# Attention's output projection by seven block products of eight, and the order of the rotation of q, k and v

## The chip, the cores and the metric

One core of one Trainium2 chip runs the whole program. The metric is the device time in microseconds (us) from start to end of one execution. The engines are PE (TensorE, the matrix products), ACT (ScalarE), DVE (VectorE), POOL (GpSimd) and SP (SyncE, which only issues DMA transfers here); each runs its own list of instructions in order and waits on the others through semaphores.

## The reference

Two sequences of 512 tokens with 1024 features go through two layers. The first mixes by a Fourier transform, the second by attention; each is followed by an MLP with squared ReLU. The part that matters here is the second layer's attention:

```python
def gqa_attention(h, w_qkv, q_gain, k_gain, w_o):
    qkv = h @ w_qkv
    q, k, v = split(qkv)     # 8 heads of q, 2 of k and v, 128 wide
    q = axial_rope(rms_norm(q, q_gain)) * HEAD_DIM ** -0.5
    k = axial_rope(rms_norm(k, k_gain))
    p = softmax(q @ k.T)               # per head, 512 x 512
    o = p @ v
    return o @ w_o           # the output projection, 1024 x 1024

x = x + gqa_attention(rms_norm(x, attn_norm), ...)
x = x + sq_relu_mlp(rms_norm(x, mlp_norm), w_up, w_down)
```

## The kernel before

**Precision.** Every float32 operand of a product is split into two float32r halves: ACT casts the high half, DVE subtracts it to get the low half (`split`, lines 84 to 86). A product of two split operands is three matmuls, high by high, high by low, low by high (`mm3`, lines 79 to 82, and `product`, line 801). All matmuls spoken of here have 128 rows, 128 columns and a moving side of 512.

**Buffers.** Five raw buffers of 512 KB take weights as they come from memory (`rawp`); four `w` buffers of 1 MB hold split weights (`wp`); 38 slots of 512 KB hold everything between stages (`act`, tiles named `u` in the profile); eight temporaries of 256 KB are named `t`; PE writes into eight PSUM banks named `ps`.

**Order.** Where the text says nothing else, a planner orders each engine's list: it takes the instructions in program order as priority and puts out those that are ready by its own costs, buffers included. Inside `tc.manual_schedule(engines=...)` the named engines keep program order.

**q, k and v** (from line 1385). Three column groups of `w_qkv`, in the order 2 (k and v), 0, 1 (q), by two sequences by four tiles of 128 tokens; each tile is 24 matmuls into one bank (`qkv`). For a tile ACT empties the bank (lines 1410, 1415), `norm_rope` (line 1301) squares each head with an accumulated sum (`head_squares`), takes the root in a chain of small DVE and ACT steps, then scales each head on ACT into a new tile (line 1315), multiplies by the two rotation tables on DVE (lines 1321, 1324) and adds on POOL (line 1326). All of that is written tile by tile: the whole of one tile's `norm_rope` stands before the next tile's. The four weights of a column group are loaded by SP into raw buffers and split (`load_w`), two of them into `w` buffers and two into slots (`lent`). The last two tiles of the last group are worked on during the first heads of attention.

**Attention** (from line 1421). For each of 16 heads (8 of each sequence): `scores` (12 matmuls, row maximum on DVE, exponential on ACT, scaling on POOL), `transpose_p` (16 transposes, then a split per bank), `values` (12 matmuls, then the head's output is split into `oT`). The next head's scores stand between the transposes of this one. During heads 6, 8, 10 and 12 the first four rows of `w_o` are loaded and split.

**Output projection** (from line 1451). For each half of the heads, for each sequence, for each of eight output blocks, `project` (line 785) makes 12 matmuls and DVE adds the bank to the residual (line 791). The residual of both sequences comes back from memory (`load_xs` from `park`). In the second half each finished block is squared on ACT (line 160) and added up on POOL (line 164), multiplied by the next norm's gain (line 206) and put away again (line 193). `blocks.root(0)` then sums the squares by small matmuls (line 172), `blocks.spread(0)` makes rows of the roots, and `blocks.first` and `first_lo` make the first operands of the second MLP.

**The second MLP** already uses the same form of block product that the change brings to the projection: `Blocks` holds 2 x 2 blocks (half of the features by sequence) under the names `b11`, `b21`, `b22`, `t1` to `t4`, and `second_sums` forms them.

## Time and profile before

The times shown are three runs and one profiled execution, all of the same kernel.

| | us |
|---|---|
| median of 3 runs | 1705.6 (1704.97 to 1710.73) |
| profiled execution | 1707.82 |
| its span in the profile | 1706.0 |
| PE busy | 1672.2 |
| DVE busy | 1233.7 |
| ACT busy | 866.0 |
| POOL busy | 358.1 |

The span is the time from the first to the last instruction that the profile shows; the execution's own time has a little around it. A row of a group names the line, the engine, the operation, output and input tiles, shapes, how many there were, the busy time, the mean duration of one in ns, and the idle time before them with what ended it. In a row of the order of time the first two numbers are start and length in us. The MATMUL rows overlap: PE starts the next before the last has ended. A row of waits reads: who waited, for whom, us in total, times, the longest.

### The profile page before, as it was taken

What the parts mean: (1) busy time and instruction counts of PE and PEld (TensorE: products, weight loads), DVE (VectorE), ACT (ScalarE), POOL (GpSimd) and SP (SyncE); (2) the same over time, 40 slices, a digit from 0 to 9 for tenths busy, and PEclk for the clock granted to TensorE, in tenths of its full rate; (3) what the DMA queues carried; (4) which work ended last, traced back from release to release, by engine and by line L of the source; (5) the groups of instructions that cost most, each with busy time, mean ns of one, the idle gap of its engine ahead of it and who ended that gap; (6) DMA issues with size and microseconds to landing.
All of it is one profiled execution on the core that took longest, in us unless ns stands there. A gap on an engine that the chain in (4) does not pass through costs nothing. (4 is left out here: it accounts for less than half of the span.)

```text
span 1706.0 us, 22195 instructions
## 1 busy us (share of the span) xinstructions
PE 1672.2 (98%) x7874; PEld 1393.4 (82%) x7874; DVE 1233.7 (72%) x1848; ACT 866.0 (51%) x1532; POOL 358.1 (21%) x332
## 2 busy tenths in 40 slices
PE   5999999999999999999999999999999999999998
PEld 4988888888888888788877888888888888887887
DVE  7869777546886869875588834687855477878875
ACT  6766445446443425456687714564444563433334
POOL 1320443231000001322234302103432220000002
PEclk8999999999999999999999999999999999999999
DMA  8652555449864757421000212234544696756632
GB/s 275 166 210 96 188 189 185 161 170 334 302 220 154 239 176 232 176 85 46 26 26 1 100 50 111 105 127 145 206 159 148 208 376 202 238 160 214 186 107 99
DMA packets 112863, 281.46 MB, mean 165 GB/s; under 512 B 11480, under 2 KB 12632, under 8 KB 112752
## 3 DMA queue, kind: packets, MB, share of 16 engines
q1 hardware_dynamic: 91520, 238.87, 39.7%
q0 software_dynamic: 6976, 15.21, 4.9%
q10 hardware_dynamic: 14256, 25.96, 4.0%
q8 instruction: 62, 1.02, 0.2%
q14 instruction: 49, 0.40, 0.1%
HBM read 204.96 MB, written 73.99 MB: 164 GB/s over the span
## 5 line engine op out<-in xcount | busy, mean ns | idle before, releaser
L807 PE MATMUL ps<-u,w 128*128 128x512 f32 x4656 | 1065.6, 389 | 2.2 <-DVE w L86 1.4
L807 PEld LDWEIGHTS ps<-u,w 128*128 128x128 f32 x4656 | 872.6, 188 | 186.8 <-DVE w L86 2.5
L85 ACT CAST w<-raw 128x1024 fp32r<-128x1024 f32 (+1 forms) x224 | 218.1, 980 | 342.6 <-PE ps L807 232.5
L86 DVE TENSOR_TENSOR w<-raw,w 128x1024 fp32r<-128x1024 f32 (+1 forms) x224 | 261.2, 1170 | 83.0 <-ACT w L85 82.7
L86 DVE TENSOR_TENSOR u<-u,u 128x1024 fp32r<-128x1024 f32 x134 | 161.3, 1232 | 18.1 <-ACT u L85 17.8
L85 ACT CAST u<-u 128x1024 fp32r<-128x1024 f32 x134 | 134.6, 1046 | 76.6 <-PE ps L807 38.1
L80 PE MATMUL ps<-u,u 128*128 128x512 f32 (+2 forms) x424 | 162.8, 385 | 2.5 <-DVE u L86 1.6
L81 PE MATMUL ps<-u,u 128*128 128x512 f32 (+2 forms) x424 | 157.3, 371 | 1.1 <-DVE u L86 1.0
L82 PE MATMUL ps<-u,u 128*128 128x512 f32 (+2 forms) x424 | 157.6, 372 | 0.4 <-DVE u L407 0.4
L1012 DVE TENSOR_TENSOR u<-ps,u 128x512 f32<-128x512 f32 x160 | 109.3, 685 | 36.6 <-PE ps L807 33.9
L807 PE MATMUL ps<-u,u 128*128 128x512 f32 x552 | 132.3, 390 | 1.9 <-DVE t L891 1.6
L922 POOL TENSOR_TENSOR u<-u 128x512 f32<-128x512 f32 x28 | 36.8, 1313 | 430.6 <-ACT u L821 430.6
L1041 POOL DMA_DIRECT2D raw<-w_sum x32 | 27.9, 873 | 470.0 <-DMA raw<-w_sum 155.5
L807 PEld LDWEIGHTS ps<-u,u 128*128 128x128 f32 x552 | 103.4, 188 | 24.5 <-issue 2.4
L164 POOL TENSOR_TENSOR t<-t,t 128x512 f32<-128x512 f32 (+1 forms) x52 | 76.3, 1473 | 202.5 <-ACT t L160 147.0
L820 ACT ACTIVATE t<-t 128x512 f32<-128x512 f32 x64 | 40.5, 632 | 112.9 <-DVE t L891 99.7
L80 PEld LDWEIGHTS ps<-u,u 128*128 128x128 f32 x424 | 82.8, 195 | 14.8 <-DVE u L86 2.0
L82 PEld LDWEIGHTS ps<-u,u 128*128 128x128 f32 x424 | 82.4, 194 | 14.0 <-DVE u L407 0.8
L81 PEld LDWEIGHTS ps<-u,u 128*128 128x128 f32 x424 | 82.8, 195 | 13.0 <-DVE u L86 2.9
L86 DVE TENSOR_TENSOR u<-ps,u 128x512 fp32r<-128x512 f32 (+4 forms) x126 | 76.6, 627 | 16.5 <-ACT u L85 15.2
L85 ACT CAST u<-ps 128x512 fp32r<-128x512 f32 (+4 forms) x126 | 66.2, 543 | 22.3 <-PE ps L82 13.7
L791 DVE TENSOR_TENSOR u<-ps,u 128x512 f32<-128x512 f32 (+1 forms) x48 | 30.9, 644 | 59.6 <-PE ps L82 59.6
(219 smaller groups left out, 1995.9 us busy)
## 6 DMA issues: line engine op xcount, KB each, us to landing
raw<-w_up SPq DMA_DIRECT2D x80, 512.0 KB, 4.5
u<-spill_t SPq DMA_DIRECT2D x60, 512.0 KB, 7.2
raw<-w_sum SPq DMA_DIRECT2D x56, 512.0 KB, 5.4
u<-spill_b SPq DMA_DIRECT2D x45, 512.0 KB, 6.2
spill_t<-u SPq DMA_DIRECT2D x84, 256.0 KB, 2.0
spill_b<-t ACTq DMA_DIRECT2D x60, 256.0 KB, 4.2
raw<-w_row SPq DMA_DIRECT2D x28, 512.0 KB, 5.3
park<-u SPq DMA_DIRECT2D x24, 512.0 KB, 3.4
```

What stands on the lines that cost most here:

```text
L80: nc.tensor.matmul(out, lh, rh, start=first, stop=False)
L81: nc.tensor.matmul(out, lh, rl, start=False, stop=False)
L82: nc.tensor.matmul(out, ll, rh, start=False, stop=last)
L85: nc.scalar.copy(dst_hi, src)
L86: eng.tensor_sub(dst_lo, src, f32(dst_hi))
L164: nc.gpsimd.tensor_add(acc[q][:, :n], acc[q][:, :n], s[:, :n])
L791: nc.vector.tensor_add(x[:, :n], o[:, :n], x[:, :n])
L807: nc.tensor.matmul(o, w[x][:, sl], h[k][y], start=first and k + i == 0, stop=k == n - 1 and i == 2, skip_group_check=not first)
L820: nc.scalar.activation(t, src, AF.Relu)
L922: eng.tensor_sub(t[:, 0], b12, b11)
L1012: nc.vector.tensor_add(x, o, x)
L1041: nc.gpsimd.dma_start(s[:, 1], w[:, 3], accum_op=ALU.add)
```

## The change

The projection is seen as a product of 2 x 2 blocks: the weights by parity of the output block and half of the heads, the heads' outputs by half of the heads and sequence. Instead of eight block products it makes seven, with sums and differences of the blocks on both sides (Winograd's form of Strassen's scheme), for each of four column groups.

- **Weights.** `keep` forms four sums for each column group, splits them in place and writes both halves to memory (`kept`); it is a generator of 17 steps, and one step stands after each tile of q, k and v from the second on. `load_kept` brings them back: of its 14 tiles the first four are loaded and split as before during attention, two (`w_a22`, laid out by the host) are loaded and split in the projection, and eight come ready from `kept` straight into a `w` buffer, in two transfers each.
- **Heads' outputs.** `values` copies each output from its bank as float32 on ACT; for sequence 0 it also splits it. `plain_sums` forms and splits the other five operands.
- **Projection.** Three parts, with PE's order fixed: eight products with sequence 0's two halves, in a turning order over the column groups; twelve with t2, t3, t4; eight with t1 and b22. What several outputs share is collected in four tiles `e` and added to the residuals by POOL's adding DMA (`common`).
- **Rotation.** A tile's squares and root are issued at once, its scaling and rotation only after the next tile's squares (`turned`). The scaling now writes in place, which frees one temporary; the last tile before attention has a slot for it.

```diff
@@ -152,15 +152,15 @@
     def xt(q, fo):
         return xs[q, fo // 2][:, fo % 2]
 
-    def square(q, fo, n=512, alone=False):
-
-        if fo == 0:
+    def square(q, fo, n=512, alone=False, first=0):
+
+        if fo == first:
             acc[q] = tm()
-        s = tm() if fo else acc[q]
+        s = acc[q] if fo == first else tm()
         nc.scalar.activation(s[:, :n], xt(q, fo)[:, :n], AF.Square)
         if alone:
             apart[q] = s
-        elif fo:
+        elif fo != first:
             nc.gpsimd.tensor_add(acc[q][:, :n], acc[q][:, :n], s[:, :n])
 
     def sums(q, n=NT):
@@ -201,7 +201,7 @@
             self.g0, self.f, self.r, self.rows, self.b = g0, {}, {}, {}, {}
 
         def gain(self, q, fo):
-            if fo % 2 == 0:
+            if (q, fo // 2) not in self.f:
                 self.f[q, fo // 2] = slot([P, 2, 512], F32)
             nc.scalar.activation(self.f[q, fo // 2][:, fo % 2], xt(q, fo), AF.Copy,
                                  scale=gc[:, self.g0 + fo : self.g0 + fo + 1])
@@ -233,6 +233,34 @@
         def first_lo(self, i):
             h = self.b["b11" if i < 2 else "b21"][i % 2]
             nc.vector.tensor_sub(h[1], self.f[0, i], f32(h[0]))
+
+        def plain_sums(self):
+
+            f, t1, t2 = self.f, [], []
+            for c in range(2):
+                t1.append(slot([P, 2, 512], F32))
+                t2.append(slot([P, 2, 512], F32))
+                nc.vector.tensor_sub(t1[c], f[1, c], f[0, c])
+                nc.vector.tensor_sub(t2[c], f[1, 2 + c], t1[c])
+                self.put("t2", t2[c])
+                yield
+            for c in range(2):
+                nc.vector.tensor_sub(f[1, c], f[1, 2 + c], f[1, c])
+                self.put("t3", f[1, c])
+                yield
+            for c in range(2):
+                nc.vector.tensor_sub(f[0, 2 + c], f[0, 2 + c], t2[c])
+                self.put("t4", f[0, 2 + c])
+                yield
+            for c in range(2):
+                self.put("t1", t1[c])
+                yield
+            for c in range(2):
+                self.put("b22", f[1, 2 + c])
+                yield
+
+        def operand(self, name):
+            return [(h[0][:, i], h[1][:, i]) for h in self.b[name] for i in range(2)]
 
         def second_sums(self):
 
@@ -808,8 +836,7 @@
                                  stop=k == n - 1 and i == 2, skip_group_check=not first)
 
     def first_product(l, blocks, rows, ahead):
-        def b(name):
-            return [(h[0][:, i], h[1][:, i]) for h in blocks.b[name] for i in range(2)]
+        b = blocks.operand
 
         def put(op, p, src, queue):
             for g, (p0, n) in enumerate(GROUPS[l]):
@@ -1310,10 +1337,10 @@
         yield
         for h0 in range(0, n, step):
             t = ts[h0 // nh]
-            x, t1, t2 = [tm((P, step, HD)) for _ in range(3)]
+            t1, t2 = [tm((P, step, HD)) for _ in range(2)]
+            x = raw[:, h0 * HD : (h0 + step) * HD].rearrange("p (h d) -> p h d", h=step)
             for i in range(step):
-                nc.scalar.activation(x[:, i], raw[:, (h0 + i) * HD : (h0 + i + 1) * HD],
-                                     AF.Copy, scale=r[:, h0 + i : h0 + i + 1])
+                nc.scalar.activation(x[:, i], x[:, i], AF.Copy, scale=r[:, h0 + i : h0 + i + 1])
 
             def every(ap):
                 return ap.unsqueeze(1).broadcast_to([P, step, ap.shape[-1]])
@@ -1327,7 +1354,8 @@
                                      t1[:, i : i + 2], t2[:, i : i + 2])
             yield
 
-    vt, kr, kT, qr, oT = {}, {}, {}, {}, {}
+    vt, kr, kT, qr = {}, {}, {}, {}
+    heads_out, ahead = Blocks(None), []
 
     def transpose_k(q):
         for h in range(NKV):
@@ -1375,15 +1403,83 @@
         for sc in range(NT):
             vh, vl = vt[q][0][:, sc, c : c + HD], vt[q][1][:, sc, c : c + HD]
             mm3(o, vh, vl, pts[sc][:, 0], pts[sc][:, 1], sc == 0, sc == NT - 1)
-        t = slot([P, 2, 512], F32R)
-        split(t[:, 0], t[:, 1], o)
-        oT[q, h] = t
+        i, j = h // 2, h % 2
+        name = "b11" if h < 4 else "b21"
+        if j == 0:
+            heads_out.f[q, i] = slot([P, 2, 512], F32)
+            if q == 0:
+                heads_out.b.setdefault(name, []).append([slot([P, 2, 512], F32R) for _ in range(2)])
+        nc.scalar.copy(heads_out.f[q, i][:, j], o)
+        if q == 0:
+            hi, lo = heads_out.b[name][-1]
+            split(hi[:, j], lo[:, j], o)
+
+
+
+    kept = [drm.tile([4, P, 2, 512], F32, name=f"kept_{m}") for m in range(4)]
+
+    def load_parts(m):
+        r = [rawp.tile([P, 1024], F32R, tag="raw", name=nm("raw")) for _ in range(2)]
+        for i in range(2):
+            nc.sync.dma_start(f32(r[i]), w_o[m, 1 - i])
+        return r
+
+    def keep():
+
+        r = load_parts(0)
+        yield
+        for m in range(4):
+            x1, x2, y1, y2 = [x[:, i : i + 512] for x in r for i in (0, 512)]
+
+            def put(i, x):
+                h = tm((P, 512), F32R)
+                split_in_place(h, x)
+                nc.sync.dma_start(kept[m][i][:, 0], f32(h))
+                nc.gpsimd.dma_start(kept[m][i][:, 1], f32(x))
+
+            def add(out, a, b, op=ALU.subtract):
+                nc.vector.tensor_tensor(out=f32(out), in0=f32(a), in1=f32(b), op=op)
+
+            add(y1, y1, x1)
+            add(x1, x1, x2, ALU.add)
+            put(0, x1)
+            yield
+            add(x2, x2, y1)
+            put(2, y1)
+            yield
+            add(y2, y2, x2)
+            put(1, x2)
+            yield
+            put(3, y2)
+            if m < 3:
+                r = load_parts(m + 1)
+            yield
+
+    def split_in_place(h, x):
+        nc.scalar.copy(h, f32(x))
+        nc.vector.tensor_sub(x, f32(x), f32(h))
+
+    def load_kept():
+
+        i = len(ahead)
+        if i < 4:
+            w = load_w(w_o[i, 0], nc.vector, 2)
+        elif i in (8, 9):
+            w = load_w(w_a22[i - 8])
+        else:
+            t = wp.tile([P, 2, 1024], F32R, tag="w", name=nm("w"))
+            for j in range(2):
+                m, k = (2 * (i % 2) + j, i // 2 - 1) if i < 8 else (i - 10, 3 * j)
+                nc.sync.dma_start(f32(t)[:, :, j * 512 : j * 512 + 512], kept[m][k])
+            w = t[:, 0], t[:, 1]
+        ahead.append([(w[0][:, i : i + 512], w[1][:, i : i + 512]) for i in (0, 512)])
 
 
     transposes = {(2, 1, 3): 0, (0, 0, 3): 1}
 
     begun = [qkv(2, 0, t, wkv, 0, KC - 2) for t in range(NT)]
     token_scale(0)
+    keeping, turned = keep(), iter(())
     for cg in (2, 0, 1):
         ws = wkv if cg == 2 else [load_w(w_qkv[cg, u], home=own if u < 2 else lent) for u in range(4)]
         for q in range(NSEQ):
@@ -1411,11 +1507,15 @@
                     split_scaled(vt[q][0][:, t], vt[q][1][:, t], o[:, 256:], r)
                     todo = norm_rope(raw, NKV, rt["k"], [t], [kr[q][:, t]])
                 else:
-                    raw = tm()
+                    raw = slot([P, 512], F32) if (cg, q, t) == (1, 1, 1) else tm()
                     nc.scalar.activation(raw, o, AF.Copy, scale=r)
                     todo = norm_rope(raw, 4, rt["q"], [t], [qr[q, 2 * cg + i][:, t] for i in range(2)])
-                for _ in todo:
+                next(todo)
+                for _ in turned:
                     pass
+                turned = todo
+                if cg != 2 or q or t:
+                    next(keeping, None)
 
 
     heads = [(q, h) for q in range(NSEQ) for h in range(NH)]
@@ -1425,11 +1525,13 @@
     nc.scalar.activation(raw[:, :512], o, AF.Copy, scale=rs[1][:, 2:3])
     head_squares(raw, 0, 4, ss)
     qT = transpose_q(*heads[1])
+    for _ in turned:
+        pass
     o = qkv(1, 1, 3, ws)
     nc.scalar.activation(raw[:, 512:], o, AF.Copy, scale=rs[1][:, 3:4])
     todo = norm_rope(raw, 4, rt["q"], [2, 3], [qr[1, 2 + i][:, t] for t in (2, 3) for i in range(2)],
                      ss, 2, nc.gpsimd)
-    ahead = []
+    assert next(keeping, 0) == 0
     for n in range(1, len(heads) + 1):
         pts, nxt = [], []
         for t in range(NT):
@@ -1446,32 +1548,83 @@
             head_squares(raw, 4, 4, ss)
         probs = nxt
         if n in (6, 8, 10, 12):
-            ahead.append(load_w(w_o[len(ahead)], nc.vector, 2))
+            load_kept()
 
     blocks = Blocks(2 * KC)
     nc.scalar.activation(one[:, :1], last[:, :1], AF.Sqrt)
-    for kh in range(2):
-        ahead += [load_w(w_o[k], home=lent) for k in range(len(ahead), 4 * kh + 4)]
-        ws = ahead[4 * kh :]
-        for q in range(NSEQ):
-            if kh == 0:
-                load_xs(q, park[q])
-            for fo in range(KC):
-                project(q, fo, ws, [(oT[q, 4 * kh + k][:, 0], oT[q, 4 * kh + k][:, 1]) for k in range(4)])
-                if kh == 0:
-                    continue
-                square(q, fo, alone=(q, fo) == (0, KC - 1))
-                blocks.gain(q, fo)
-                if fo % 2:
-                    put_away(q, fo // 2)
-                if (q, fo) == (1, 0):
-                    blocks.root(0)
-                if (q, fo) == (1, 2):
-                    blocks.spread(0)
-                if (1, 2) < (q, fo) < (1, 7):
-                    blocks.first(fo - 3)
-                if (q, fo) > (1, 3):
-                    blocks.first_lo(fo - 4)
+
+
+    todo, e = heads_out.plain_sums(), [tm() for _ in range(4)]
+    load_xs(0, park[0])
+
+    def add(x, o):
+        nc.vector.tensor_add(x, o, x)
+
+    def common(m, *xs):
+        for x in xs:
+            nc.gpsimd.dma_start(x, e[m], accum_op=ALU.add)
+
+    def turn(*steps):
+
+        for i in range(5):
+            if i < 4:
+                yield i, 0
+            if i:
+                yield i - 1, 1
+
+    with tc.manual_schedule(engines={ET.PE}):
+        o = {}
+        for m, i in turn():
+            if i == 0:
+                o[m] = ps()
+            product(o[m], ahead[m][i], heads_out.operand(("b11", "b21")[i]), i == 0)
+            if i:
+                add(xs[0, m][:, 0], o[m])
+                load_kept()
+            else:
+                nc.scalar.copy(e[m], o[m])
+            if m + i > 1:
+                next(todo)
+        load_xs(1, park[1])
+        for k, name in enumerate(("t2", "t3", "t4")):
+            h = heads_out.operand(name)
+            for m in range(4):
+                o = ps()
+                product(o, ahead[4 + 2 * k + m // 2][m % 2], h)
+                if k < 2:
+                    add(e[m], o)
+                    common(m, *((xs[1, m][:, 0],), (xs[0, m][:, 1], xs[1, m][:, 1]))[k])
+                else:
+                    add(xs[0, m][:, 1], o)
+                if k:
+                    fo = 2 * m + k - 1
+                    square(0, fo, alone=fo == KC - 1)
+                if k == 2:
+                    blocks.gain(0, 2 * m)
+                    blocks.gain(0, 2 * m + 1)
+                    put_away(0, m)
+                if m % 2:
+                    load_kept()
+                next(todo, None)
+        o = {}
+        for j, (m, i) in enumerate(turn()):
+            if i == 0:
+                o[m] = ps()
+            product(o[m], ahead[10 + m][i], heads_out.operand(("t1", "b22")[i]), i == 0)
+            fo = 2 * m + 1 - i
+            add(xt(1, fo), o[m])
+            square(1, fo, first=1)
+            blocks.gain(1, fo)
+            if i:
+                put_away(1, m)
+            if j == 0:
+                blocks.root(0)
+            if j == 2:
+                blocks.spread(0)
+            if 1 < j < 6:
+                blocks.first(j - 2)
+            if 2 < j < 7:
+                blocks.first_lo(j - 3)
     second_product(1, blocks, ())
     ats = []
     for f in range(2 * PLAIN):
@@ -1711,7 +1864,7 @@
...
-        "w_o": i["attn_w_o"][0].reshape(KC, P, D),
+        "w_o": i["attn_w_o"][0].reshape(2, 4, P, 4, 2, P).transpose(3, 4, 2, 0, 1, 5).reshape(4, 2, P, 1024),
+    arrays["w_a22"] = arrays["w_o"][:, 1, :, 512:].reshape(2, 2, P, 512).transpose(0, 2, 1, 3).reshape(2, P, 1024)
```

4 lines of the change are left out of this document (2 added, 2 removed).

## The prediction

> **What bounds the kernel now.** I read the page's head first, then the waits of TensorE (PE) from the end of the first MLP to the start of the second, then the busy time by stage, and last the order of time at the seams.
>
> ```profile
> span 1706.0 us, 22195 instructions
> PE 1672.2 (98%) x7874; PEld 1393.4 (82%) x7874; DVE 1233.7 (72%) x1848; ACT 866.0 (51%) x1532; POOL 358.1 (21%) x332
> ...
> PE ps L81 <- DVE u L86: 1.0, 3, 0.5
> PE ps L80 <- ACT u L85: 0.3, 1, 0.3
> PE ps L1367 <- POOL t L1361: 0.2, 1, 0.2
> ...
> 739.00:766.00 27.00, 27.00 (x128) 22.55 (x127) 18.69 (x75) 17.24 (x68) 4.41 (x6) 1.00 0.06 20
> 766.00:858.00 92.00, 92.00 (x415) 76.23 (x414) 54.32 (x167) 63.58 (x239) 26.11 (x34) 1.00 0.10 35
> 858.00:870.00 12.00, 12.00 (x70) 10.03 (x69) 10.37 (x22) 9.62 (x22) 3.52 (x5) 1.00 0.27 89
> 870.00:900.00 30.00, 28.83 (x154) 22.46 (x153) 25.30 (x60) 26.06 (x66) 13.05 (x19) 1.00 0.01 1
> 900.00:930.00 30.00, 29.64 (x166) 23.81 (x166) 26.59 (x57) 23.22 (x55) 12.88 (x20) 1.00 0.00 1
> 930.00:967.00 37.00, 37.00 (x211) 31.08 (x210) 30.90 (x67) 28.65 (x68) 13.10 (x19) 1.00 0.11 33
> 981.00:1073.00 92.00, 92.00 (x417) 76.41 (x416) 44.05 (x59) 31.79 (x48) 15.81 (x11) 1.00 0.22 80
> ```
>
> Columns of the stages: stretch, length, busy us of PE, PEld, DVE, ACT, POOL, granted clock, DMA share, GB/s. The first two rows are q, k and v, the next four attention, the last the output projection. PE is never idle in q, k, v and the projection, at clock 1.00, and loses 1.17 and 0.36 us in two stretches of attention. So a matmul taken out of the projection shortens the end by its whole slot, unless something else comes late; work taken off DVE or ACT there is worth nothing by itself.
>
> **What is removed.** The projection has 2 halves x 2 sequences x 8 outputs x 4 heads x 3 = 384 matmuls. The new form has 4 column groups x 7 products x 4 x 3 = 336, of the same shape: 48 fewer.
>
> ```profile
> 1046.11 0.39 PE L80 MATMUL ps<-u,u 128*128 128x512 f32 x1
> ...
> 1051.32 0.39 PE L82 MATMUL ps<-u,u 128*128 128x512 f32 x1
> ```
>
> From the first to the second of these lie 23 matmul steps: 5.21 / 23 = 0.2265 us a slot (the 0.39 overlaps its neighbours). 48 x 0.2265 = **10.9 us** off the path; with 12 matmuls a product takes 2.72 us.
>
> **What is added in q, k and v.** For each of four column groups: two loads of 512 KB, four DVE sums, four ACT casts, four DVE remainders, four writes of 256 KB on SP's queue and four on POOL's.
>
> ```profile
> 1037.57 0.68 DVE L859 TENSOR_TENSOR raw<-raw,raw 128x512 f32<-128x512 f32 x1
> 809.16 0.61 ACT L85 CAST w<-raw 128x512 fp32r<-128x512 f32 x1
> L1041 POOL DMA_DIRECT2D raw<-w_sum x32: 858/868/907, 418.1 to 1607.5; - x32
> ```
>
> 32 x 0.68 = 21.8 us of DVE, 16 x 0.61 = 9.8 of ACT, 16 x 0.868 = 13.9 of POOL. The first two stage rows hold 119 us; there DVE goes from 73.0 to 94.8 (80%), ACT from 80.8 to 90.6 (76%), POOL from 30.5 to 44.4. PE waits for none of it: it only needs its bank emptied by one ACT copy a tile, and eight banks stand against one tile every 24 x 0.2265 = 5.4 us. I cost it at nothing; the cover is those banks and PE's full row. The rotation put behind the next tile's squares issues the same instructions 5.4 us later, fills ACT's and DVE's waits for each other, and gains nothing, since PE has no idle time there to win.
>
> The seam is where the weights of the next column group must be ready, because the sums now share the five raw buffers and SP's queue with them.
>
> ```profile
> L94 SPq DMA_DIRECT2D raw<-w_qkv x8: 328/328/382, 694.0 to 735.4; - x8
> ...
> 764.59 1.37 DVE L86 TENSOR_TENSOR u<-raw,u 128x1024 fp32r<-128x1024 f32 x1
> 766.85 1.23 DVE L86 TENSOR_TENSOR u<-raw,u 128x1024 fp32r<-128x1024 f32 x1 [0.41 <-ACT u L85]
> ...
> 769.43 0.39 PE L80 MATMUL ps<-u,u 128*128 128x512 f32 x1
> 770.79 0.39 PE L80 MATMUL ps<-u,u 128*128 128x512 f32 x1
> ...
> raw<-w_o SPq DMA_DIRECT2D x8, 512.0 KB, 4.3
> L85 ACT CAST u<-u 128x1024 fp32r<-128x1024 f32 x134 | 134.6, 1046 | 76.6 <-PE ps L807 38.1
> L86 DVE TENSOR_TENSOR u<-u,u 128x1024 fp32r<-128x1024 f32 x134 | 161.3, 1232 | 18.1 <-ACT u L85 17.8
> ```
>
> The third and fourth weights are split at 764.59 + 1.37 = 765.96 and 768.08 and used at 769.43 and 770.79: 3.5 and 2.7 us to spare, with raws that lay ready since before 740. Parts 0 and 1 stand ahead of these loads in the program and take four buffers. If a buffer comes free only when part 0 is written away, some 765 by its place after the sixth tile, the last weight takes 4.3 + 1.05 + 1.23 = 6.6 more and another 4 us behind the load ahead of it: about 776, **5 us** late. I take 0, since the sums can run in the gaps of DVE after 739 (18.69 of 27 busy), long before 760; bounds 0 and 5.
>
> **What is added in attention.** Each head's output is also copied by ACT; for sequence 1 that copy replaces the split.
>
> ```profile
> L85 ACT CAST u<-ps 128x512 fp32r<-128x512 f32 x21 | 11.5, 589 | 1.6 <-PE ps L82 1.1 <-PE ps L1367 0.6
> L86 DVE TENSOR_TENSOR u<-ps,u 128x512 fp32r<-128x512 f32 x22 | 14.4, 679 | 0.4
> ```
>
> Eight copies x 0.589 = 4.7 us more of ACT for sequence 0; 8 x 0.679 = 5.4 us less of DVE for sequence 1, where PE hardly waits. One tile's rotation also moves into 858 to 870. Of the two idle stretches the one with ACT at 26.06 of 30 loses 1.17, the one at 23.22 loses 0.36: 0.81 us for 2.84 us of ACT. A stretch of 30 us holds about 3.9 heads (7.7 us each), so 2.3 us more ACT: 2.3 x 0.81 / 2.84 = 0.66 a stretch, 1.3 for two; less for the freed third buffer of a rotation. I take **+1.0**; bounds -1.5 (today's idle time goes) and +4.7 (each copy shifts PE in full).
>
> **The projection itself.** PE's order is now fixed by hand.
>
> ```profile
> 979.33 1.64 PE L1367 MATMUL ps<-ident,t 128*128 128x128 f32 x13 [0.23 <-POOL t L1361]
> ...
> 981.04 0.39 PE L80 MATMUL ps<-u,w 128*128 128x512 f32 x1
> ...
> L791 DVE TENSOR_TENSOR u<-ps,u 128x512 f32<-128x512 f32 x31 | 21.4, 689 | 39.4 <-PE ps L82 39.4
> 1063.48 2.35 DVE L219 TENSOR_TENSOR u<-u,t 128x1024 f32<-128x1024 f32 x2
> L164 POOL TENSOR_TENSOR t<-t,t x12: 1286/1292/2269, 1034.2 to 1073.5; 128x512 f32<-128x512 f32 x12
> ```
>
> Now one projection matmul (981.04) slips in between the last head's; after, it can't, so the last head's splits may show: **+0.3**, bounds 0 and 0.9. DVE: 44.05, less 8 PSUM adds of 0.689, plus 8 sums of 1.18 and 10 splits of 1.23, less two weight splits: 57.8 of 81 us. ACT: 31.79 + 10 x 1.05 + 4 copies of 0.59 - 2 x 1.05 = 42.6. Both fit. The first eight products need only sequence 0's halves, split during attention: 21.7 us in which the two pairs of t2 take 4 x 1.18 + 2 x 1.23 = 7.2 of DVE. Each later operand has four products (10.9 us). Weights come ready from memory into four buffers: a tile is issued when its buffer's last product ends, five products (13.6 us) ahead at first, six (16.3) later; two halves at 4.3 each land well within that.
>
> The sums of squares of sequence 0 now stand one product behind its last output: its add and square take 0.69 + 0.63, and POOL's eight issues and six adds in the two phases before need 8 x 0.87 + 6 x 1.29 = 14.7 of 21.8 us. **+0.3**, bounds 0 and 1.7 (below).
>
> [...]
>
> **Sum**: -10.9 + 0 + 1.0 + 0.3 + 0.3 = -9.3 us. The profiled execution took 1707.82 with its span at 1706.0; the span should become 1696.7, the rest around it stays. The median of the three runs is 1705.6, 2.2 below that execution: 1705.6 - 9.3 = **1696.3 us**.
>
> **Rivals.**
> Clean (0.14): nothing new shows and attention's 1.5 us goes too: 1705.6 - 12.4 = 1693.2, up to 1695. For: DVE is freed in the later heads. Against: ACT is fuller where PE waits.
> Attention pays in full (0.11): 4.7 in place of 1.0 gives 1700.0. For: ACT at 87% before the change. Against: the copy isn't what PE waits for.
> The raw ring (0.05): 5 us at the seam, 1701.3. Against: the sums can run early.
> POOL late (0.04): each of the six adds takes 2.27, so the last adding transfer, due 10.9 + 0.7 us into the two phases, is issued 6 x 0.98 = 5.9 later and out at 18.4; landing after 6.5 (row below) it is there at 24.9, add and square end at 26.2, and the sums of squares that PE holds at 24.5 wait 1.7 in place of 0.3: 1697.7. Against: the median add of that stretch takes 1.292.
> The change doesn't do what it says (0.04): half of the weight sums isn't done in q, k and v but slides into 858 to 930, where DVE has 72 - 62.3 = 9.7 us free for 10.9 more; if PE waits for all of it, 1707.2. Against: they come first in the program.
>
> The one that ends on the other side (0.08) is the traffic of the projection.
>
> ```profile
> L150 SPq DMA_DIRECT2D u<-park x8: 319/323/1261, 961.7 to 970.8; - x8
> ...
> DMA to landing us min/median/max: 2.6/6.1/12.1
> ...
> raw<-w_sum POOLq DMA_DIRECT2D x28, 256.0 KB, 6.5
> ```
>
> The stage moved 80 GB/s x 92 us = 7.4 MB; now come 8 tiles of 1.05 MB, 1.05 MB of a22, 3.1 MB of sums added by DMA and the parked 4.2 MB if late: 24 MB in 81 us, some 300 GB/s. If the halves of a tile land one behind the other at the longest time of a parked block, 2 x 12.1 = 24.2 us, PE waits 24.2 - 13.6 = 10.6 at the first turn of the buffers and 24.2 - 16.3 = 7.9 at the second: 1696.3 + 18.5 = 1714.8. It begins above 13.6 us a tile and eats the gain at (9.3 + 29.9) / 2 = 19.6. For: much more traffic; against: the median 6.1 makes 12.2, under 13.6. [...]
>
> **How the numbers follow.** The forecast holds 0.54 (its own range 1695 to 1698). The range leaves out the traffic rival, the sliding sums and a little below: **1693 to 1704**. A change of 0.5% is 8.5 us, about what a measurement can tell from none: faster means under 1697.1, which is the clean case and 0.42 of the forecast's 0.54: 0.56. Slower means over 1714.1, the traffic rival: 0.08. The rest, 0.36, is the same.
>
> **What would show it.** The projection's stretch should be 81 us with PE full, no DMA among PE's waits; q, k and v PE-full with DVE near 80%; attention's idle near 3 us; the sums' writes over before 858. It is wrong if PE waits for a weight at a group's start or a kept tile in the projection, or if another stretch loses time.

## The result, and the profile after

The changed kernel takes 1714.39 us (median of five runs, 1712.67 to 1715.42); the kernel before took 1705.61 beside it. The ratio is 1.0042, 95% interval 1.0026 to 1.0059: slower by a little under half a per cent. The forecast was 1696.3, its range 1693 to 1704, so the time lies outside the range and on the other side of the kernel before. In the profiled execution the span went from 1706.0 to 1713.0, where 1696.7 was expected: 16.3 us are to be found.

The head of the page after:

```profile
span 1713.0 us, 22359 instructions
PE 1666.6 (97%) x7826; PEld 1386.3 (81%) x7826; DVE 1260.9 (74%) x1880; ACT 885.6 (52%) x1568; POOL 384.1 (22%) x360
```

PE has the 48 matmuls less (7874 to 7826), but its busy time fell by 5.6 us only, where 10.9 was expected, although its span grew. What PE waited for from 700 to 1250 us, after the change (who, for whom, us in total, times, the longest):

```profile
PE ps L80 <- ACT u L85: 3.2, 1, 3.2
PE ps L835 <- DVE w L86: 2.7, 2, 1.6
PE ps L172 <- POOL t L164: 2.0, 1, 2.0
PE ps L1395 <- POOL t L1389: 1.5, 1, 1.5
PE ps L835 <- DVE t L918: 1.3, 1, 1.3
PE ps L172 <- ACT t L160: 1.3, 1, 1.3
```

With the small ones below these it is 14.8 us; before, the same view adds up to 3.5. Four of the six are new: the split of head 1's queries (L80), which PE needs for the scores that stand ahead of head 0's transposes, and head 0's softmax (L1395), both at the start of attention, and two waits of the small matmuls that sum the squares (L172) in the projection. The L86 group holds a wait of 1.64 us for the second MLP's first weights, which is new as well.

The stages after the change (stretch, length, busy PE, PEld, DVE, ACT, POOL, granted clock, DMA share, GB/s):

```profile
768.00:860.00 92.00, 92.00 (x415) 76.05 (x413) 68.56 (x179) 65.40 (x234) 32.14 (x41) 1.00 0.46 159
860.00:872.00 12.00, 7.08 (x24) 4.95 (x24) 8.99 (x18) 10.44 (x29) 6.29 (x7) 0.72 0.19 61
...
864.80:871.60 6.80, 5.26 (x20) 3.94 (x19) 6.80 (x13) 5.46 (x18) 4.35 (x5) 0.51 0.28 87
...
985.00:1070.00 85.00, 81.58 (x362) 67.47 (x361) 45.43 (x57) 37.10 (x57) 23.34 (x23) 0.96 0.69 210
...
1052.50:1059.30 6.80, 6.80 (x23) 6.01 (x24) 0.68 (x4) 2.00 (x5) 0.00 (x0) 0.51 0.85 304
```

q, k and v are as the forecast had them: PE full, with the weight sums beside it. The loss lies behind them. With each of the two new pairs of waits the granted clock is about one half for 6.8 us, and there one matmul follows the other after 0.43 us (867.90 to 868.33) in place of 0.23. The second stretch, with PE busy throughout, loses 3.4 us by that; the first begins behind the wait for the split and has the wait of 1.5 us inside it, so that PE is busy for 5.26 us only and loses 2.6. The account of the span is then: -10.9 for the matmuls, +11.3 for waits (14.8 - 3.5), +6.0 for the two stretches at half clock, together +6.4; the span grew by 7.0. The same can be read from how far PE is behind the kernel before at the same instruction:

| PE's instruction | before | after | behind |
|---|---|---|---|
| first transpose of the keys, early in q, k and v | 760.34 | 762.01 | 1.7 |
| second head's first transpose | 866.76 | 876.62 | 9.9 |
| last head's first transpose | 978.15 | 986.51 | 8.4 |
| sums of squares of sequence 1, in the second MLP | 1092.07 | 1099.00 | 6.9 |

So 8.2 us go at attention's start, and the projection, where 10.9 us were taken out, brings PE only 1.5 nearer. The first 1.7 us lie ahead of the changed stages; what they come from wasn't followed up.

**Attention's start.** ACT's list before and after, around the last whole tile of q (start, length, instruction, and in brackets the idle time ahead of it):

```profile
843.13 1.28 ACT L1315 ACTIVATE t<-t,s 128x128 f32<-128x128 f32 x4 [1.09 <-DVE s L140]
844.45 0.69 ACT L1415 ACTIVATE t<-ps,rs 128x512 f32<-128x512 f32 x1
...
850.66 1.28 ACT L1359 ACT_TABLE_LOAD   x1
```

```profile
853.23 1.28 ACT L1343 ACTIVATE t<-t,s 128x128 f32<-128x128 f32 x4 [1.10 <-DVE s L140]
854.41 0.66 ACT L1511 ACTIVATE u<-ps,rs 128x512 f32<-128x512 f32 x1
...
858.28 1.28 ACT L1343 ACTIVATE u<-u,s 128x128 f32<-128x128 f32 x4 [1.15 <-DVE s L140]
...
860.16 1.28 ACT L1387 ACT_TABLE_LOAD   x1
861.45 0.69 ACT L1387 ACTIVATE t<-ps,s 128x512 f32<-128x512 f32 x1
```

The exponentials' table comes 9.5 us later than before; PE was behind by 1.7 of that early in q, k and v and lost nothing in them. Head 1's split stands behind the second exponential, at 862.79, and PE waits for it from 860.2. Note the order: each scaling (L1343) waits for the root of its own tile (L140) and stands **ahead of** the next tile's evacuation, although the code now issues it behind the next tile's squares. The planner put it there by its own costs.

**The projection.** DVE's list near the end of the sums of squares, with the issue on POOL of the transfer that its last row waits for, and the transfers of 985 to 1075 us (issues, KB each, median us to landing), after; the last fence is the row of before for the parked blocks:

```profile
1035.18 0.69 DVE L1561 TENSOR_TENSOR t<-ps,t 128x512 f32<-128x512 f32 x1 [2.03 <-PE ps L835]
...
1042.42 0.88 POOL L1565 DMA_DIRECT2D u<-t  x1 [1.12 <-issue]
...
1045.62 0.69 DVE L1561 TENSOR_TENSOR u<-ps,u 128x512 f32<-128x512 f32 x1 [4.30 <-DMA u<-t]
1051.05 1.29 DVE L1561 TENSOR_TENSOR u<-ps,u 128x512 f32<-128x512 f32 x2 [4.74 <-DMA u<-t]
```

```profile
DMA  0000000753989999998999999999999940057004
...
w<-kept SPq DMA_DIRECT2D x16, 512.0 KB, 6.5
u<-t POOLq DMA_DIRECT2D x12, 256.0 KB, 7.5
park<-u SPq DMA_DIRECT2D x6, 512.0 KB, 7.8
```

```profile
park<-u SPq DMA_DIRECT2D x8, 512.0 KB, 2.6
```

The twelve adding transfers (`u<-t`) bring what several outputs share into the residuals, and DVE's last additions wait 4.30 and 4.74 us for them. From 1007.5 to 1057 us the DMA engines are nine tenths busy or more in 20 of 22 slices, and the parked blocks need three times as long as before. PE waits for no kept tile; what comes late is the chain add, square, sum. The landing is only a part of it. The shared part that the last of these transfers but one brings is ready on DVE at 1035.87 (1035.18 + 0.69); POOL issues the transfer at 1042.42, 6.5 us later, and it lands 8.5 us after that, at 1050.95. Each of the last five is issued 0.3 us after the third one before it has landed (1042.12 for this one), so one slow landing delays the issue of the next.

### The profile page after: what moved, and what is told of

Its sections match the earlier page's. It is cut to its first block, busy times and chain, and to the rows that moved or that the text cites. A ratio compares the mean times of both kernels' runs of the same rounds, so it can differ in the third digit from the quotient of the medians.

```text
span 1713.0 us, 22359 instructions
## 1 busy us (share of the span) xinstructions
PE 1666.6 (97%) x7826; PEld 1386.3 (81%) x7826; DVE 1260.9 (74%) x1880; ACT 885.6 (52%) x1568; POOL 384.1 (22%) x360
## 4 chain that ended last, share of the span: by engine, by line
PE 42%; DVE 4%; ACT 3%; DMA 1%; issue 1%; POOL 0%; DVEq 0%; ACTq 0%; POOLq 0%
PE ps L835 34%; PE ps L81 2%; PE ps L82 2%; PE ps L80 2%; PE ps L1395 1%; DMA raw<-w_sum 1%; DVE u L86 1%; ACT t L1325 1%; DMA u<-t 0%; ACT t L1387 0%; ACT t L1343 0%; ACT u L85 0%; DVE w L86 0%; PE ps L172 0%; PE ps L1374 0%
## 5 line engine op out<-in xcount | busy, mean ns | idle before, releaser
L835 PE MATMUL ps<-u,w 128*128 128x512 f32 x4992 | 1145.2, 390 | 5.0 <-DVE w L86 2.9
L835 PEld LDWEIGHTS ps<-u,w 128*128 128x128 f32 x4992 | 936.6, 188 | 204.3 <-DVE w L86 4.7
L86 DVE TENSOR_TENSOR w<-raw,w 128x1024 fp32r<-128x1024 f32 (+1 forms) x226 | 262.5, 1166 | 82.5 <-ACT w L85 82.2
L85 ACT CAST u<-u 128x1024 fp32r<-128x1024 f32 x144 | 144.6, 1047 | 82.2 <-PE ps L835 38.9
L86 DVE TENSOR_TENSOR u<-u,u 128x1024 fp32r<-128x1024 f32 x144 | 173.3, 1231 | 16.2 <-ACT u L85 15.8
L80 PE MATMUL ps<-u,u 128*128 128x512 f32 (+2 forms) x360 | 137.1, 383 | 7.0 <-ACT u L85 3.7
L82 PE MATMUL ps<-u,u 128*128 128x512 f32 (+2 forms) x360 | 132.4, 368 | 1.0 <-DVE u L86 0.6
L81 PE MATMUL ps<-u,u 128*128 128x512 f32 (+2 forms) x360 | 131.6, 366 | 0.3 <-DVE u L86 0.3
L835 PEld LDWEIGHTS ps<-u,u 128*128 128x128 f32 x552 | 103.4, 188 | 24.5 <-issue 2.8
L80 PEld LDWEIGHTS ps<-u,u 128*128 128x128 f32 x360 | 69.8, 194 | 17.5 <-ACT u L85 4.4
L82 PEld LDWEIGHTS ps<-u,u 128*128 128x128 f32 x360 | 69.6, 193 | 12.5 <-DVE u L86 1.6
L81 PEld LDWEIGHTS ps<-u,u 128*128 128x128 f32 x360 | 70.0, 194 | 8.8 <-DVE u L86 0.9
L86 DVE TENSOR_TENSOR u<-ps,u 128x512 fp32r<-128x512 f32 (+4 forms) x118 | 70.7, 623 | 8.1 <-ACT u L85 7.7
L907 DVE TENSOR_TENSOR t<-ps,u 128x512 f32<-128x512 f32 x32 | 22.0, 687 | 62.0 <-PE ps L835 58.3
L160 ACT ACTIVATE t<-u 128x512 f32<-128x512 f32 (+1 forms) x64 | 37.8, 603 | 56.9 <-DVE u L1561 29.9
```

The costliest lines, as they stand in the source:

```text
L80: nc.tensor.matmul(out, lh, rh, start=first, stop=False)
L81: nc.tensor.matmul(out, lh, rl, start=False, stop=False)
L82: nc.tensor.matmul(out, ll, rh, start=False, stop=last)
L85: nc.scalar.copy(dst_hi, src)
L86: eng.tensor_sub(dst_lo, src, f32(dst_hi))
L160: nc.scalar.activation(s[:, :n], xt(q, fo)[:, :n], AF.Square)
```

## The experiments

Two causes were suspected from the trace: that ACT's chain in q, k and v carries over into attention, and that the traffic of the projection delays the adding transfers. Each expectation names its own theories for these. Every ratio below is to the kernel before on the same chip, with its 95% interval; the changed kernel's is 1.0042.

**1. Sums for one column group of four** (`one_group`; the other groups use these sums too, so the kernel leaves out three quarters of them and computes something else):

```diff
-        for m in range(4):
+        for m in range(1):
...
-                nc.sync.dma_start(f32(t)[:, :, j * 512 : j * 512 + 512], kept[m][k])
+                nc.sync.dma_start(f32(t)[:, :, j * 512 : j * 512 + 512], kept[0][k])
```

> The changed kernel, but the weight sums are formed for the first of the four column groups only (the kept tiles of that group are read four times, so the output isn't the reference's): 12 casts, 24 DVE operations and 24 writes less in q, k and v. Theory (ACT falls behind PE in q, k and v by the casts, and the first exponentials of attention pay for it): PE's 3.2 and 1.5 us waits at the start of attention and the 6.8 us of half clock behind them go, some 7 to 8 us less than the changed kernel's 1714.4, about 1706.5. Rival (the rotation moved into attention's start delays the exponentials): the waits stay, about 1714.

Measured 1.0008 (0.9999 to 1.0017). Neither the wait for head 1's split nor the half clock behind it is left. The gain is 5.8 us of the 7 to 8 expected: the projection's waits grew from 2.0 and 1.3 to 2.8 and 1.5, and a wait of 1.9 us for a rotated key (L1364), with 3.4 us at half clock behind it, is new in q, k and v. The weight sums cause attention's loss.

**2. The rotation back in its place** (`rotation_back`):

```diff
-                next(todo)
-                for _ in turned:
+                for _ in todo:
                     pass
-                turned = todo
```

> The changed kernel with a tile's rotation directly behind its own squares again, the weight sums as they are. Theory (the planner had put the rotation ahead of the next tile's squares anyhow): same, 1713 to 1716, with the waits at the start of attention as they are. Rival (the moved rotation of the last tile delays the first exponentials): 5 to 8 us less, 1706 to 1709.

Measured 1.0127 (1.0111 to 1.0143): neither theory had this. PE's waits from 742 to 900 us:

```profile
PE ps L80 <- ACT u L85: 12.4, 3, 10.4
PE ps L1364 <- DVE s L134: 3.2, 1, 3.2
```

One wait of 10.4 us now stands ahead of attention, with the granted clock at one half for 13.7 us behind it; three more stretches at half clock, of 3.4, 3.4 and 10.2 us, stand elsewhere (mean granted clock of the run 0.990, in the kernel after 0.994). Beside the sums, the moved rotation is worth 1.0127 - 1.0042 = 0.0085, 14.5 us.

**3 and 4. The adding transfers** (`adds_on_dve`: DVE adds, no transfer; `half_loads`: the adding transfers stay, but each kept tile brings only its first half, which is then used for both column halves, so the kernel computes something else):

```diff
-            nc.gpsimd.dma_start(x, e[m], accum_op=ALU.add)
+            nc.vector.tensor_add(x, e[m], x)
```

```diff
-            for j in range(2):
+            for j in range(1):
...
-        ahead.append([(w[0][:, i : i + 512], w[1][:, i : i + 512]) for i in (0, 512)])
+        ahead.append([(w[0][:, c : c + 512], w[1][:, c : c + 512]) for c in ((0, 512) if i < 4 or i in (8, 9) else (0, 0))])
```

> The changed kernel with the twelve additions of the shared part into the residuals as DVE additions in place of POOL's adding transfers; same output. Theory (the adding transfers land late among the loads, DVE's last additions wait for them, the sums of squares wait for those and the clock is halved for 6.8 us): PE's waits of 2.0 and 1.3 us before the sums, the half clock and most of the 0.7 and 1.6 us behind them go, 7 to 9 us less, 1705.5 to 1707.5. Rival (DVE and POOL are late by their own work in the projection): within 2 us of 1714, since DVE gets 8 us more.

> The changed kernel with half of the bytes of the kept weights: each of the eight kept tiles loads its first half only and uses it for both of its column groups (the output isn't the reference's), 8 transfers of 512 KB less. Theory (the adding transfers are late because the transfer engines are full): they land in half the time, PE's waits before the sums go, 6 to 9 us less, 1705.5 to 1708.5. Rival (the adding transfers are slow by themselves or by POOL's ring): 1713 to 1715.

Measured 0.9996 (0.9987 to 1.0005) for both. In both the waits of L172 and the half clock behind them are gone, while attention's start stays as it was (the wait for the split is 3.91 us in both). Either less traffic or no adding transfer cures the place: the adding transfers are late because of the traffic beside them. In `half_loads` they don't land in half the time, as its theory had it (6.1 us in the median against 7.5), but the earlier landings let the next ones be issued earlier: the one of 1042.42 is issued at 1039.55 and has landed at 1047.14. 1.0042 - 0.9996 is 7.9 us; the waits and the half clock there were 2.0 + 1.3 + 3.4 = 6.7.

**5 to 8. ACT's work, and the second MLP's first weights.** On `adds_on_dve`, `keep`'s casts go to GpSimd or to VectorE; `_rows` loads two weight rows of the second MLP ahead of the projection's last eight products.

```diff
-        nc.scalar.copy(h, f32(x))
+        nc.gpsimd.tensor_copy(h, f32(x))
```

```diff
+        early_rows = [halves(load_raw(w_up[1, 2 * p]), home=lent) for p in range(2)]
...
-    second_product(1, blocks, ())
+    second_product(1, blocks, early_rows)
```

> The changed kernel with the twelve additions on DVE, and the sixteen casts of the weight sums on POOL in place of ACT; same output. Theory (ACT's sixteen casts are what puts it behind PE at the end of q, k and v): PE's two waits at the start of attention and the half clock behind them go; adds_on_dve stood at ratio 0.9996, so 8 us less: 0.995. Rival (it is DVE's sums and remainders, 21.8 us, that put the chain behind): as adds_on_dve, 0.999 to 1.000.

> The same with the casts on DVE. Theory: ACT catches up and the waits go, 0.995; DVE gets about 16 x 0.4 to 0.7 us more, so a part may come back. Rival (DVE is what is late): slower than adds_on_dve, above 1.000.

> cast_on_pool, and the first two weights of the second MLP's first products are split into slots before the projection's last eight products, not into buffers that these free. Theory: the waits of 0.7 and 1.6 us at the start of the second MLP go as well, 2 us under cast_on_pool, ratio 0.9935. Rival (the splits take DVE's time from the norms that PE needs at the same place): no less than cast_on_pool.

> adds_on_dve with the two weights split early in the same way, casts on ACT as in the changed kernel. Theory: 2 us under adds_on_dve, ratio 0.9984, with PE's waits at the start of attention as they are (3.9 and 1.4 us). Rival: no less than 0.9996.

Measured: casts on GpSimd 1.0036 (1.0023 to 1.005), with the early rows 1.0035 (1.0022 to 1.0047); casts on VectorE 1.0013 (1.0004 to 1.0021); early rows alone 0.9984 (0.9975 to 0.9993). The three with casts moved lie far from what was expected, and tell the most. With the casts on GpSimd, the stage row of q, k and v, then PE's largest wait from 742 to 900 us, then ACT's from 768 to 860:

```profile
768.00:860.00 92.00, 88.62 (x385) 71.65 (x384) 69.17 (x169) 55.81 (x210) 40.15 (x50) 0.98 0.50 160
```

```profile
PE ps L80 <- ACT u L85: 4.5, 2, 3.9
```

```profile
ACT t L1343 <- DVE s L140: 23.3, 12, 4.1
```

ACT's busy time there fell from 65.40 to 55.81 us, and the wait for head 1's split is no shorter (3.9). The time came back as waits of ACT for the root on DVE. With the casts on VectorE the wait for the split is 1.7 us, but PE waits 3.5 us in q, k and v for splits on VectorE. Less work on ACT doesn't bring it in time, then, if what it waits for comes later. ACT's own waits in the kernel before (766 to 858 us) and after (768 to 860) say the same:

```profile
ACT t L1315 <- DVE s L140: 19.4, 16, 2.1
ACT s L135 <- DVE s L134: 5.7, 13, 0.7
ACT t L1415 <- PE ps L82: 1.4, 3, 0.6
```

```profile
ACT t L1343 <- DVE s L140: 17.1, 12, 2.5
ACT s L135 <- DVE s L134: 4.8, 6, 2.3
```

Before, ACT was busy for 63.58 of these 92 us, but for another 25.1 it waited for DVE's small steps, and only 1.4 was time in which it waited for PE. So the chain of ACT and DVE was nearly as long as PE's time before the change already, and the change put 16 casts of 0.61 us into it, and weight sums of 0.69 ahead of DVE's small steps. No run takes the sums off DVE and leaves the casts on ACT, so the share of each in the delay isn't shown.

**9 to 13. ACT in the code's order.** If it is the order, ACT held to the code's (evacuate, square, then the tile before's scaling) should start attention in time. `act_in_order` does it in the changed kernel, `both_cures` with the additions on VectorE and the early rows, `both_cures_earlier` from four tiles further ahead; the two `weights_first` also spread the next column group's weight loads over the tiles before.

```diff
+    in_order = tc.manual_schedule(engines={ET.Activation})
...
+                if (cg, q, t) == (1, 1, 0):
+                    in_order.__enter__()
...
+    in_order.__exit__(None, None, None)
```

```diff
-        ws = wkv if cg == 2 else [load_w(w_qkv[cg, u], home=own if u < 2 else lent) for u in range(4)]
+        ws, coming = wkv if cg == 2 else coming, []
...
+                if cg != 1 and q:
+                    coming.append(load_w(w_qkv[{2: 0, 0: 1}[cg], t], home=own if t < 2 else lent))
```

> The changed kernel with ScalarE held to the order in which the code issues its work, from the first tile of the last q,k,v group of tiles (cg 1, q 1) to the split of head 1's q; nothing else is changed, so that the evacuations, the squares and head 0's exponentials no longer stand behind a rotation that waits for its own tile's root. Theory A (the order of ScalarE's chain, not its amount of work, makes attention start late): the waits of 3.21 and 1.54 us at the start of attention and the 6.8 us at half clock behind them go, together 3.21 + 1.54 + 3.4 = 8.15 us or 0.0048 of the time; as with one group of sums, where the same waits went, about a quarter comes back in longer waits of the projection's sums, so 1.0042 - 0.0034, a ratio of 1.0008 (1.000 to 1.002). Rival (ScalarE has too much work there in any order): head 0's first transpose stays near 865 us and the ratio near 1.004.

> The version with the additions on VectorE and two early weight rows of MLP-2, and with it ScalarE in the code's order from the first tile of (cg 1, q 1) on. Theory A: 0.9984 less (3.23 + 1.43 + 3.4) / 1707 = 0.0047, a ratio of 0.9937 (0.993 to 0.995), PE without a wait over 1 us between 720 and 1060 us and no half clock there. Rival (too much work in any order): 0.9984. Rival (the time comes back at the projection, as with one group of sums): about 0.996.

> As the run before, but with ScalarE in the code's order from the first tile of (cg 1, q 0), four tiles earlier. If ScalarE's lateness is gathered over the whole group, this starts attention earlier than holding the last two tiles alone, by what the other still waits there; if that one waits for nothing, the two agree within 0.001. If the order held too early makes weight casts late, PE waits in q, k and v and the ratio lies above it.

> As act_in_order, with the four loads of the next column group's weights issued one after each tile of (q 1) in the group before, since there ScalarE in the code's order made these weights late (PE waited 3.98 us at 767.5 and 5.15 us at 820.2 for casts of w, with 17 us at half clock behind them). Nothing else is changed. Theory A (the order of ScalarE's chain is what attention's start costs): these waits go too, the starts of attention and of q, k and v are both free of waits, and the ratio is that of the changed kernel less up to 8.15 us, with some 2 us given back at the projection's sums: 1.0008 (0.999 to 1.002). Rival (ScalarE's work with the weights' casts is too much in any order): waits of some us stay in q, k and v or come back at attention's start, and the ratio is 1.004 or more.

> As both_cures (additions on VectorE, two early weight rows of MLP-2, ScalarE in the code's order), with the next column group's weights loaded one after each tile of the group before. Theory A: 0.9984 less 8.06 us of 1707, a ratio of 0.9937 (0.993 to 0.996), and no wait of PE over 1 us between 720 and 1225 us. Rival (too much work for ScalarE in any order): 0.998 or more.

Measured 1.0094 (1.0079 to 1.011), 1.0037 (1.0025 to 1.005), 1.0036 (1.0024 to 1.0049), 1.0076 (1.0063 to 1.009) and 1.0028 (1.0017 to 1.0039): `both_cures_earlier` agrees with `both_cures`, which was one of its cases, and the other four are slower than expected. In `both_cures`, ACT's list before attention (the last tile's evacuation), and PE's waits from 742 to 1060 us:

```profile
861.45 0.69 ACT L1514 ACTIVATE u<-ps,rs 128x512 f32<-128x512 f32 x1 [1.78 <-PE ps L82]
```

```profile
PE ps L80 <- ACT w L85: 9.1, 2, 5.2
PE ps L81 <- DVE w L86: 1.7, 2, 1.1
```

ACT now waits 1.78 us for PE at a tile, so in this order it keeps pace, and no wait is left at attention's start. But the column groups' weights, which the code loads at the start of a group, were cast late: 9.1 us. Both of these waits (from 767.0 and 818.7) stand ahead of the part that `both_cures` marks, and `both_cures_earlier` has the same two; so the planner seems to have kept ACT's whole list of this stage in the code's order. Loading the weights earlier in the code didn't help enough; in `both_cures_weights_first` SP's loads waited 19.2 us in all for writes of `kept` to free a raw buffer. These runs show ACT in time at attention's start, but not what that is worth.

**14 to 16. Two scalings off ACT.** The order is left to the planner; the scaling of the last two tiles ahead of attention (`scale_on_pool`, `both_cures_pool`) or of the six of the last column group (`both_cures_pool_four`) is one GpSimd product.

```diff
+            if scale is nc.gpsimd:
+                nc.gpsimd.tensor_mul(x, x, r[:, h0 : h0 + step].unsqueeze(2).broadcast_to([P, step, HD]))
-            for i in range(step):
+            for i in range(step if scale is nc.scalar else 0):
                 nc.scalar.activation(x[:, i], x[:, i], AF.Copy, scale=r[:, h0 + i : h0 + i + 1])
...
+                                     scale=nc.gpsimd if (cg, q) == (1, 1) else nc.scalar)
```

> The changed kernel with the scaling of the last two rotations ahead of attention, of the tiles (1, 1, 0) and (1, 1, 1), on GpSimd as one broadcast product each in place of four ScalarE activations; the order of everything else stays the scheduler's. ScalarE then stands before head 0's exponentials without two scalings and the waits for their roots: 2 x (1.28 + 1.14) = 4.8 us less. Theory A (the chain of ScalarE through its own waits for the root is what makes the exponentials late): the wait of 3.21 us at 860 and the half clock behind it (3.4 us) go, and the wait of 1.54 us for the softmax's POOL shrinks: 1.0042 less 6.6 to 8.1 us with a quarter given back at the projection's sums, 1.001 (1.000 to 1.002). Rival (the amount of work, or another engine behind ScalarE, VectorE or GpSimd, is as late): head 0's first transpose stays within 1 us of 865 and the ratio near 1.004.

> The same on the version with the additions on VectorE and two early weight rows of MLP-2. Theory A: 0.9984 less (3.23 + 3.4) to (3.23 + 1.43 + 3.4) us of 1707, a ratio of 0.994 (0.993 to 0.9955), PE without a wait over 1 us between 720 and 1220 us. Rival (amount of work, or another engine): 0.998.

> As both_cures_pool, with the scaling of all six tiles of column group 1 ahead of attention (four of q 0, two of q 1) on GpSimd. If two tiles already bring ScalarE back to PE's pace, this is the same within 0.001; if not, attention starts earlier by what was left. [...]

Measured 1.001 (1.0001 to 1.0019), as its theory A expected; 0.9957 (0.9945 to 0.997), just above its 0.993 to 0.9955; and 0.994 (0.9927 to 0.9954), 1698.49 against 1708.06 us. `scale_on_pool` moves eight ACT activations and nothing else, and the wait for the split is gone, where sixteen casts less had left it. What is left of attention's start is one wait of 1.7 us for the softmax on GpSimd. In the last of the three, ACT's list at head 0's first exponential, the stages, and PE's largest waits from 700 to 1250 us:

```profile
855.38 0.69 ACT L1389 ACTIVATE t<-ps,s 128x512 f32<-128x512 f32 x1 [0.42 <-DVE s L1387]
```

```profile
768.00:860.00 92.00, 91.97 (x415) 75.80 (x413) 70.38 (x185) 62.49 (x226) 40.30 (x50) 1.00 0.45 153
860.00:872.00 12.00, 10.29 (x54) 7.79 (x55) 11.14 (x23) 10.30 (x26) 6.11 (x7) 1.00 0.30 89
...
985.00:1070.00 85.00, 84.27 (x381) 69.42 (x379) 63.70 (x74) 44.90 (x63) 18.98 (x13) 1.00 0.57 202
```

```profile
PE ps L835 <- DVE w L86: 1.2, 1, 1.2
PE ps L1397 <- POOL t L1391: 1.2, 1, 1.2
```

The exponential comes 6.1 us earlier than at 861.45 (4.8 of them if counted from the keys' first transpose, 760.69 here), the clock is 1.00 in all three stages, and no wait is above 1.2 us. This version beats both kernels, and its gain of 9.6 us is close to what the forecast had for the change by itself (9.3), though made up of other terms. It is the change with the additions on VectorE, the early rows and six scalings on GpSimd; what the last two would be worth in the kernel before wasn't run.

How late ACT is can be read without PE's waits, from the keys' first transpose to the load of the exponentials' table. In the kernel before this takes 90.3 us. In the four versions whose q, k and v are those of the change (the kernel after, runs 3, 4 and 8) it takes 98.1 to 101.0; with one group of sums 94.3, with two scalings off ACT 95.1, with six 93.0; but with the casts on GpSimd 106.4 and on VectorE 101.8. So taking 9.7 us of casts off ACT made it no earlier in either place, while two scalings of 1.28 us, with the waits in front of them, made it some 3 us earlier.

## Why the prediction was wrong, by its own steps

- **The matmuls, -10.9: right in the main.** They have to be read where nothing else is late. From the last head's first transpose to the sums of root(1) the kernel before takes 113.9 us, and the version with both causes cured 104.0, 0.7 of it one wait of PE, so 10.0 of the 10.9 us are there:

```profile
978.15 0.27 PE L1367 MATMUL ps<-ident,t 128*128 128x128 f32 x1
...
1092.07 0.95 PE L172 MATMUL ps<-ones,t 128*128 128x2 f32 x8
```

```profile
979.95 2.23 PE L1397 MATMUL ps<-ident,t 128*128 128x128 f32 x16
...
1083.90 0.95 PE L172 MATMUL ps<-ones,t 128*128 128x2 f32 x8
```

- **The sums in q, k and v: the step that failed first.** "I cost it at nothing; the cover is those banks and PE's full row." The cover is real as far as it goes: PE stays full in q, k and v. But the banks hide a late ACT only as long as PE has tiles of q to go on with; attention's first head needs ACT at once, and there the lateness is paid. It came to 3.2 + 1.5 us of waits and 2.6 at half clock, 7.3 us of the 8.2 by which PE falls back there, where the sum had 0 and, for this, no bound above it. The rival "the sums slide into attention" looked at the right place, but the sums were over by then; it was ACT that slid. The step read the busy shares (ACT 76%) as room, although ACT had filled the rest with waits for DVE's small steps and waited for PE for only 1.4 of 92 us.
- **"Gains nothing, since PE has no idle time there to win": wrong.** Run 2 puts the moved rotation at 14.5 us beside the sums. The forecast judged it by the kernel before, where PE doesn't wait, and not by the kernel that it is put into.
- **The sums of squares, +0.3 with bounds 0 and 1.7: mis-sized.** 2.0 + 1.3 us of waits and 3.4 at half clock, 6.7 us. The rival "POOL late" had the place and the transfer, but took a landing of 6.5 us and doubted only POOL's adds. Its 2.27 us for each of the six isn't shown: in the kernel after, they took 1.28 to 1.29 us each for the first three and 4.32 together for the last three. The transfer that DVE's last addition waits for landed after 8.5 us, and it was issued 6.5 us after its operand was ready, because it stood behind the landings of earlier ones; that wait was in no term.
- **The traffic rival** names 1714.8, which is near the measured time, by another way: PE waits for no kept tile (they land after 6.5 us in the median, where the forecast had 13.6 to spare). The traffic does its harm through the adding transfers; runs 3 and 4 show that: with fewer bytes, or without these transfers, the waits go.
- **The second MLP's first weights** have no term in the sum. 1.64 us of PE's wait for them went with two early rows (run 8: 0.9984 beside 0.9996 without them).
- **Attention itself, +1.0: the wrong sign.** From the second head to the last the kernel after gained 1.5 us on the one before (9.9 us behind, then 8.4), which is the lower of the bounds -1.5 and +4.7. ACT's added copies cost nothing that shows. The raw ring's 0 holds: PE waits for no weight in q, k and v. The last head's +0.3 shows as no wait.
- **The clock** isn't in the sum at all: the two pairs of waits cost 6.0 us (2.6 + 3.4) beyond their length.

So the mechanism by which the change gains was right, and two chains that feed PE, ACT with DVE and the adding transfers, were priced by busy time and landing time and not by what they wait for.

## What to carry to other kernels

The idle share of an engine's row isn't its room. ACT, idle for 30% of q, k and v, waited there for DVE's small steps, and for PE only 1.4 us in 92; 9.7 us of casts moved off it gained nothing, while two scalings that waited in its chain gained 5.5 us (1.0042 against 1.001). The wait for the bottleneck engine is a sign of room, not a measure of it: in the best version ACT waits for PE not at all from 768 to 860 us and still starts attention in time. What tells is when the engine reaches the first thing that PE needs. Where one stage's cover ends (here at attention's first head) the lateness gathered under it is paid at once, and with it a stretch at half clock (6.8 us at 0.51 in the kernel after); so the first user behind the seam is what to look at. A transfer whose result the next engine needs at once doesn't belong in a stretch in which the DMA engines are already nine tenths busy (the adding transfers landed after 7.5 us here in the median), and the time from ready to issue (6.5 us for one of them) counts as well as the landing.

## What the runs showed of the hardware

In these runs the granted clock fell to one half after short waits of PE. In the kernel after, a wait of 3.2 us was followed by 6.8 us at a clock of 0.5 (the 0.51 of the first window above), and so was a pair of 2.0 and 1.3 us; a single wait of 1.93 us in run 1 was followed by 3.4 us, the one of 10.4 us in run 2 by 13.7. A wait's length alone doesn't decide it: a wait of 1.7 us at the same place was followed by 6.8 us at half clock in `both_cures_pool` (granted 0.51 from 862.6 to 869.4) and by none in `scale_on_pool` (1.00 from 860 to 872). In the first 45 us of the program, where PE does the same in both, the kernel before had 6.8 and 3.4 us at half clock (from 22.9 and 39.9) among waits of 2.8, 0.9, 0.7 and 0.8 us, and the kernel after none among 2.7, 0.7, 0.7 and 0.8. What else decides it isn't shown.

In the kernel after, POOL had at most three adding transfers under way: the last five were each issued 0.3 us after the landing of the third one before. What sets this isn't shown.

Moving a waiting instruction mattered more here than moving work. GpSimd took 1.04 us for a scaling (`both_cures_pool`, at 852.37 and 856.94) that took ACT 1.28 (four activations, in the kernel after). `scale_on_pool` gains 0.0032 or 5.5 us over the kernel after by two of these; some 3 us of it is ACT's earlier start, and the half clock that no longer comes at attention's start (2.6 us) makes up most of the rest.
